# Squares of the attention output for three of four heads on GpSimd and VectorE instead of ScalarE, with the norm's chain issued in the next head's first unit

## Chip, cores, metric

The kernel runs on one core of a Trainium2 chip. The metric is the time of one execution on the device in microseconds (us); runs are compared by their median. TensorE (PE in the profile) multiplies matrices and transposes, VectorE (DVE), ScalarE (ACT) and GpSimd (POOL) do the elementwise work, SyncE (SP) issues most of the loads.

## The reference

Two layers. Each normalises its input, projects it, runs three groups of heads side by side (a recurrence, a gated convolution, an attention), multiplies each group's output by a gate and projects back. The change lies in the attention: 4 heads, 512 latent rows with 256 context rows, and two score matrices per head whose softmaxes are subtracted. What a head gives is normalised by the root of its mean square over the head's 128 values, and multiplied by a gate from `z`:

```python
def diff_attend(q, k, v, lam, scale):
    s = jnp.einsum('bqhjd,bkhjd->bhjqk', q, k).astype(jnp.float32) * scale
    p = jax.nn.softmax(s, axis=-1)
    attn = p[:, :, 0] - lam * p[:, :, 1]
    return jnp.einsum('bhqk,bkhe->bqhe', attn.astype(v.dtype), v)

    def finish(o, z):
        o = rms_norm(o, subln_g) * (1.0 - lam_init)
        return o.reshape(o.shape[0], o.shape[1], D_ATTN) * jax.nn.silu(z)
```

Layer 0 computes latent and context rows (768), layer 1 latent rows alone (512).

## The kernel before

The attention of a layer works through heads 0 to 3, and in each head through units of query tiles of 128 rows. Layer 0 has six tiles in five units, in the order `(0,), (4, 5), (1,), (2,), (3,)`: a unit is one latent tile against 768 keys or the two context tiles against 256 keys each. Layer 1 has four units of one tile.

The loop over units is a pipeline written out by hand. In the turn of unit u it transposes u's weights (`aT_mm` into the PSUM tile `aTp`, copied by ScalarE to `aT`), drains the output of the unit before (`drain`), makes the coefficient `cf` of the unit after it and combines that unit's two softmaxes with it (`coef`, `combine`: `e` on VectorE, and for a latent unit the 256 context columns on GpSimd, L1255 and L1256), takes the exponentials of the unit after that (`expo`), the scores `sc` and their row maxima `mx` of the one after that (`scores`, `maxi`), and multiplies u's weights by the values (`av`). TensorE's instructions, ScalarE's and those of VectorE that go through `dv` keep the order in which they are written. The small steps of the norm on VectorE and the work on GpSimd are placed between them by the tile scheduler.

`drain` copies a tile's output from PSUM to the head's tile O (L1298), and a second instruction of ScalarE squares it from PSUM and adds each row up into a column of `ss` (printed as `oss`). The squares themselves go to a tile `osq` that nobody reads.

`finish(h, O)` is the head's norm and gate, in two parts, run for head h within head h+1. Part 1 is issued at the end of the turn whose number in the head is FI: it loads the gate of the head from memory into the tile `zT`, of which there is one buffer, then makes `r0` (printed `r`), multiplies `oss` by it twice, scales, takes an inverse root (`rsqrt`: an integer estimate `rs_i`, `rs_y`, and three Newton rounds of three instructions with `rs_t`, the last result being `ors`), multiplies that by `r`, and scales O by it: on GpSimd for heads 0 to 2, on VectorE for head 3. Part 2 is issued at the end of turn FI2 = 3: TensorE transposes O into `oT`, in two groups; VectorE multiplies them by the gate in place in `zT`; ScalarE casts the result (`lat`, `ctx`), and GpSimd subtracts for the low part.

`aTp`, `av` and `oT` share two PSUM buffers. So `oT` waits for the reads of the `av` or `aTp` that had its buffer, and the `aTp` behind it for VectorE's reading of `oT`. Between these, output weights are split into high and low parts (`split`: `wo..hi` on ScalarE, `wo..lo` on GpSimd or VectorE, placed by the scheduler).

Of the kernel before, what the change touches and what calls it, by code (L numbers as in the profile page):

```python
# [10 lines left out]
F32 = mybir.dt.float32  # L11
# [3 lines left out]
ALU = mybir.AluOpType  # L15
AX = mybir.AxisListType
PSUM = bass.MemoryType.PSUM

P = 128
# [15 lines left out]
WH = 3  # L35
FSB = 3
PTB = 4
FI = 1
FK = (0,1,2,3,4,5,6,7)
HS = 0  # L40
WK = 2
# [65 lines left out]
def build(tc, A):  # L107
    nc = tc.nc
    ctx = ExitStack()
    S, G = nc.scalar, nc.gpsimd  # L110
# [17 lines left out]
    V = Vec()  # L128
# [63 lines left out]
    def small(n, tag, pool=None, bufs=2):  # L192
        return (pool or sm).tile([P, n], F32, tag=tag, bufs=bufs, name=tag)
# [5 lines left out]
    for l in range(L):  # L199
        t = cst.tile([P, NCC], F32, name=f"chan{l}")  # L200
# [260 lines left out]
    def fill(us):  # L461
        while us > 0 and fq:
            try:
                us -= next(fq[0])
            except StopIteration:
                fq.pop(0)
# [715 lines left out]
    def attention(l, lat, cx, pool, az_done, hd0):  # L1182
        last = l == L - 1
        li = 0.8 - 0.6 * math.exp(-0.3 * l)
        n = NL if last else NT
# [7 lines left out]
        ntt = 4 if last else 6  # L1193
        vA = pool.tile([P, 6, 512], F32, name="vA")
        ss = small(24, "oss", pool, 1)
# [11 lines left out]
        def dv(i):  # L1207
            order("v", i)

        def ac(i):  # L1210
            order("s", i)
# [81 lines left out]
        def drain(u):  # L1293
            for po, tt in zip(u["po"], u["tt"]):
                if AC & 4:
                    dv(V.tensor_copy(Os[u["h"]][:, tt], po))
                else:
                    ac(S.copy(Os[u["h"]][:, tt], po))  # L1298
                osq = pool.tile([P, P], F32, tag="osq", bufs=2, name="osq")
                col = u["h"] * 6 + tt  # L1300
                ac(S.activation(osq, po, AF.Square, accum_out=ss[:, col:col + 1]))

# [1 line left out]

        def finish(h, O):
            zT = pool.tile([P, NT], F32, tag="zT", bufs=ZB, name="zT")
            nc.sync.dma_start(out=zT[:, :n], in_=zd[l][h, :, :n])
            E1 = V if h == 3 else G
            c0 = h * 6
# [3 lines left out]
            for _ in range(2):  # L1313
# [6 lines left out]
                             in1=rs[:, :ntt].unsqueeze(2).to_broadcast([P, ntt, P]), op=ALU.mult)  # L1320
# [27 lines left out]
        def at(i):  # L1348
            return us[i] if 0 <= i < len(us) else None

        for x in range(-3, len(us)):
            u, p, c, e, w = at(x), at(x - 1), at(x + 1), at(x + 2), at(x + 3)
# [9 lines left out]
            if p:  # L1362
                drain(p)
# [25 lines left out]
            else:  # L1389
                fill(FA[1])  # L1390
            if u and u["i"] == FI and u["h"]:
                fins.append(finish(u["h"] - 1, Os[u["h"] - 1]))
# [82 lines left out]
    for l in range(L):  # L1475
        F.update(FL[l])
        last = l == L - 1
        n = NL if last else NT
# [248 lines left out]
```

## Time and profile before

| | |
|---|---|
| runs | 1145.35, 1146.66, 1151.25 us |
| median | 1146.66 us |
| profiled execution | 1148.92 us |
| its span in the profile | 1147.1 us |
| TensorE's mean granted clock | 0.97 of full speed |
| attention of layer 0 | about 476 to 574 us of the span |
| attention of layer 1 | about 1015 to 1094 us |

The span runs from the first to the last instruction; the 1.8 us between it and the profiled execution lie outside the instructions. Lines are read as start, duration, engine, line of the kernel, operation, tile written<-tiles read. `L118`, `L135`, `L137` and `L145` are helpers through which all of VectorE's, the matrix products' and the transposes' instructions pass, so there the tile's name tells what is done. A value in brackets is the time that the engine stood idle before the instruction, with what ended it.

### The profile page before, as it was taken

To read this page: it belongs to the slowest core of one execution; us is meant where nothing else is said; L and a number is where in the kernel's file an instruction comes from. 1 tells how busy PE (TensorE), PEld (TensorE's weight loads), DVE (VectorE), ACT (ScalarE), POOL (GpSimd) and SP (SyncE) were. 2 spreads that over 40 slices of the span, in tenths; PEclk is the share of its full clock that TensorE was granted. 3 is DMA by queue.
4 is the path that set the end of the run, shared out by engine and by line. 5 is a ranking of instruction groups with operands and counts; after the bars stand their busy time and mean duration, and the time that the engine had idled before them with its cause. 6 is when DMAs were issued, how large, how long until landed. Compare 5 with 4: busy or idle time off the path is not lost.

```text
span 1147.1 us, 25449 instructions
## 1 busy us (share of the span) xinstructions
PE 1038.8 (91%) x9850; PEld 849.6 (74%) x9850; DVE 721.3 (63%) x1704; ACT 523.4 (46%) x1330; POOL 499.2 (44%) x516
## 2 busy tenths in 40 slices
PE   4899989999799998988899998998988999888897
PEld 1577978777688867877787776866767887777775
DVE  3431458788567261589847867766885815479944
ACT  4323453453353222468724664654344433238731
POOL 1211444434726522555522345254475463456532
PEclk9889999999899999989999999999999999899999
DMA  9455231212424466653052452232223345555143
GB/s 356 174 194 167 80 89 57 57 35 70 139 75 130 139 189 187 195 170 102 15 188 80 142 186 78 84 83 76 79 71 103 103 133 149 154 164 165 47 156 110
DMA packets 92088, 142.55 MB, mean 124 GB/s; under 512 B 28192, under 2 KB 36416, under 8 KB 91968
## 3 DMA queue, kind: packets, MB, share of 16 engines
q1 hardware_dynamic: 88512, 136.14, 38.3%
q10 hardware_dynamic: 3456, 4.80, 1.2%
q8 instruction: 77, 1.26, 0.5%
q14 instruction: 43, 0.35, 0.1%
HBM read 110.99 MB, written 25.71 MB: 119 GB/s over the span
## 4 chain that ended last, share of the span: by engine, by line
PE 35%; DVE 21%; ACT 7%; POOL 6%; issue 5%; DMA 4%; SPq 1%; DVEq 0%; POOLq 0%; ACTq 0%
PE pcl L137 10%; PE op L137 6%; PE ptl L137 3%; DVE mx L118 3%; PE pcc L137 3%; PE ptc L137 2%; DVE rs_t L118 2%; POOL wlo L264 2%; PE av L137 1%; DVE e L118 1%; PE ch L135 1%; DVE bk L118 1%; DMA mraw<-in_mod_w_dram 1%; PE sc L137 1%; DMA qks<-qkr 1%
## 5 line engine op out<-in xcount | busy, mean ns | idle before, releaser
L264 POOL TENSOR_TENSOR wlo<-wraw,whi 128x512 fp32r<-128x512 f32 x134 | 182.0, 1361 | 310.4 <-ACT whi L261 265.7
L137 PE MATMUL pcl<-lat,whi 128*128 128x512 f32 (+1 forms) x928 | 300.1, 400 | 1.7 <-POOL lat L347 1.3
L137 PEld LDWEIGHTS pcl<-lat,whi 128*128 128x128 f32 x928 | 173.4, 193 | 44.1 <-issue 9.2
L137 PE MATMUL pcl<-lat,wlo 128*128 128x512 f32 (+1 forms) x464 | 187.8, 405 | 5.6 <-POOL wlo L264 3.7
L261 ACT CAST whi<-wraw 128x512 fp32r<-128x512 f32 x144 | 88.7, 619 | 159.8 <-DMA wraw<-in_w_in_dram 55.3
L137 PE MATMUL pcc<-ctx,whi 128*128 128x256 f32 x576 | 109.5, 286 | 2.0 <-DVE ctx L118 1.7
L137 PEld LDWEIGHTS pcl<-lat,wlo 128*128 128x128 f32 x464 | 89.7, 193 | 27.1 <-POOL wlo L264 5.6
L137 PEld LDWEIGHTS pcc<-ctx,whi 128*128 128x128 f32 x576 | 92.5, 192 | 8.4 <-issue 3.0
L137 PE MATMUL pcc<-ctx,wlo 128*128 128x256 f32 x288 | 83.3, 289 | 1.9 <-DVE wlo L118 1.9
L137 PE MATMUL ptl<-whi,lat 128*128 128x256 f32 x384 | 80.3, 296 | 0.0
L1244 ACT ACTIVATE e<-sc,mx 128x768 f32<-128x768 f32 (+1 forms) x80 | 66.3, 831 | 19.5 <-DVE mx L118 14.1
L118 DVE TENSOR_REDUCE mx<-sc 128x1 f32<-128x768 f32 (+1 forms) x72 | 63.7, 918 | 15.9 <-PE sc L137 15.9
L137 PE MATMUL av<-vA,aT 128*128 128x128 f32 x416 | 59.9, 288 | 14.0 <-ACT aT L1279 13.8
L137 PEld LDWEIGHTS av<-vA,aT 128*128 128x128 f32 x416 | 54.7, 197 | 20.9 <-ACT aT L1279 17.8
L137 PEld LDWEIGHTS ptl<-whi,lat 128*128 128x128 f32 x384 | 64.0, 198 | 2.0 <-issue 0.4
L137 PEld LDWEIGHTS pcc<-ctx,wlo 128*128 128x128 f32 x288 | 55.3, 192 | 5.1 <-issue 2.6
L118 DVE TENSOR_TENSOR R<-s,cs 128x384 f32<-128x384 f32 (+1 forms) x96 | 47.0, 529 | 18.6 <-PE s L135 17.8
L941 POOL TENSOR_TENSOR pz<-zu,pc 64x128 f32<-64x128 f32 x88 | 39.4, 448 | 42.1 <-DVE zu L118 37.4
L137 PE MATMUL ptl<-wlo,lat 128*128 128x256 f32 x192 | 56.5, 294 | 0.0
L137 PE MATMUL sc<-KH,QS 128*128 128x256 f32 (+1 forms) x144 | 52.0, 374 | 4.7 <-ACT e L1244 2.9
L137 PE MATMUL sc<-KL,QS 128*128 128x256 f32 (+1 forms) x144 | 45.7, 339 | 0.0
L1255 POOL TENSOR_TENSOR e<-e,cf 128x256 f32<-128x256 f32 x32 | 26.2, 819 | 42.1 <-DVE cf L118 14.1
(450 smaller groups left out, 2450.2 us busy)
## 6 DMA issues: line engine op xcount, KB each, us to landing
wraw<-in_w_in_dram SPq DMA_DIRECT2D x144, 256.0 KB, 2.7
mraw<-in_mod_w_dram SPq DMA_DIRECT2D x96, 256.0 KB, 4.3
KH<-qd SPq DMA_DIRECT2D x32, 192.0 KB, 3.9
oraw<-in_w_out_dram SPq DMA_DIRECT2D x20, 256.0 KB, 3.9
qd<-qks SPq DMA_DIRECT2D x12, 384.0 KB, 2.3
qd<-qkr SPq DMA_DIRECT2D x12, 384.0 KB, 2.5
qks<-qkr SPq DMA_DIRECT2D x64, 64.0 KB, 2.1
zu<-vd SPq DMA_DIRECT2D x96, 32.0 KB, 2.2
```

The source lines that it names most:

```text
L118: i = f(*a, **k)
L135: tc.keep_in_program_order(nc.tensor.matmul(*a, **k))
L137: i = nc.tensor.matmul(*a, **k)
L261: S.copy(hi, raw)
L264: eng.tensor_tensor(out=lo, in0=raw, in1=hi.bitcast(F32), op=ALU.subtract)
L941: G.tensor_tensor(out=pz[d][hr], in0=zu[d][hr, :, h, :], in1=prepd[d][1][hr, :, cc[d][1]].unsqueeze(2).to_broadcast([64, 2, HD]), op=ALU.mult)
L1244: ac(S.activation(ej[:, c], pb[:, c], AF.Exp, bias=mx[:, i:i + 1], accum_out=den[:, u["h"] * 6 + tt, j:j + 1]))
L1255: G.tensor_tensor(out=e1, in0=e1, in1=cf[:, 0:1].to_broadcast([P, NC]), op=ALU.mult)
```

## The change

ScalarE squares the tiles of head 3 alone. For heads 0 to 2, `finish` starts with a product of O with itself on GpSimd, written into the head's `zT`, and a sum of each 128 values on VectorE into `ss`; after these the gate is loaded into the same buffer. FI goes from 1 to 0, so part 1 is issued at the end of the next head's first turn, the one in which the head's last tile is drained. The tile `osq` has one buffer instead of two.

```diff
-FI = 1
+FI = 0
...
                 else:
                     ac(S.copy(Os[u["h"]][:, tt], po))
-                osq = pool.tile([P, P], F32, tag="osq", bufs=2, name="osq")
+                if u["h"] < 3:
+                    continue
+                osq = pool.tile([P, P], F32, tag="osq", bufs=1, name="osq")
                 col = u["h"] * 6 + tt
                 ac(S.activation(osq, po, AF.Square, accum_out=ss[:, col:col + 1]))
...
         def finish(h, O):
             zT = pool.tile([P, NT], F32, tag="zT", bufs=ZB, name="zT")
+            if h < 3:
+                sq = zT[:, :n].rearrange("p (t c) -> p t c", c=P)
+                G.tensor_tensor(out=sq, in0=O[:, :ntt], in1=O[:, :ntt], op=ALU.mult)
+                V.tensor_reduce(out=ss[:, h * 6:h * 6 + ntt], in_=sq, axis=AX.X, op=ALU.add)
             nc.sync.dma_start(out=zT[:, :n], in_=zd[l][h, :, :n])
             E1 = V if h == 3 else G
```

In numbers: 30 squares of 128x128 with their accumulator reads leave ScalarE (18 in layer 0, 12 in layer 1), and GpSimd gets six products and VectorE six sums (three over 128x768, three over 128x512).

The scheduler places some instructions anew. VectorE at the start of head 2 of layer 0, before (`oss` is the sum of squares, `e` with x2 the combine of the unit of two context tiles, `r` the reciprocal):

```order
L118 RECIPROCAL cf<-oden 128x2
L118 SCALAR_TENSOR_TENSOR cf<-cf,lm_579,oden 128x2
L118 TENSOR_TENSOR oss<-oss,r_6473 128x6
L118 SCALAR_TENSOR_TENSOR e_6363<-e_6377,cf,e_6363 128x256 x2
L118 TENSOR_TENSOR oss<-oss,r_6473 128x6
L118 TENSOR_SCALAR oss<-oss 128x6
L118 TENSOR_SCALAR rs_i<-oss 128x6
L118 TENSOR_SCALAR rs_y<-rs_i 128x6
L118 TENSOR_TENSOR rs_t<-rs_y 128x6
L118 TENSOR_REDUCE mx<-sc 128x1 x2
```

and now:

```order
L118 RECIPROCAL cf<-oden 128x2
L118 SCALAR_TENSOR_TENSOR cf<-cf,lm_579,oden 128x2
L118 SCALAR_TENSOR_TENSOR e_6343<-e_6357,cf,e_6343 128x256 x2
L118 TENSOR_REDUCE oss<-zT 128x6
L118 TENSOR_REDUCE mx<-sc 128x1 x2
L118 TENSOR_TENSOR oss<-oss,r_6413 128x6
L118 RECIPROCAL cf<-oden 128x1
L118 TENSOR_TENSOR oss<-oss,r_6413 128x6
```

The sum of the squares stands between the combine and the row maxima; the five steps that stood ahead of the maxima come behind them.

VectorE at the end of the same head, before (`e_6520` is the combine of its fifth unit, `e_6562` that of the next head's first; the numbers of buffers differ between the two kernels):

```order
L118 TENSOR_REDUCE mx<-sc 128x1
L118 TENSOR_TENSOR ors<-ors,r_6473 128x6
L118 TENSOR_REDUCE mx<-sc 128x1
L118 RECIPROCAL cf<-oden 128x1
L118 RECIPROCAL r_6732<-oden 128x6
L118 SCALAR_TENSOR_TENSOR cf<-cf,lm_579,oden 128x1
L118 SCALAR_TENSOR_TENSOR e_6520<-e_6533,cf,e_6520 128x512
L118 TENSOR_REDUCE mx<-sc 128x2 x2
L118 RECIPROCAL cf<-oden 128x1
L118 SCALAR_TENSOR_TENSOR cf<-cf,lm_579,oden 128x1
L118 TENSOR_TENSOR zT<-oT,zT 128x384
L118 SCALAR_TENSOR_TENSOR e_6562<-e_6577,cf,e_6562 128x512
```

and now, with `e_6494` for the fifth unit and `e_6534` for the next head's first:

```order
L118 SCALAR_TENSOR_TENSOR e_6494<-e_6507,cf,e_6494 128x512
L118 SCALAR_TENSOR_TENSOR ors<-rs_t,rs_y 128x6
L118 TENSOR_REDUCE mx<-sc 128x2
L118 TENSOR_TENSOR ors<-ors,r_6413 128x6
L118 TENSOR_REDUCE mx<-sc 128x2
L118 RECIPROCAL cf<-oden 128x1
L118 SCALAR_TENSOR_TENSOR cf<-cf,lm_579,oden 128x1
L118 SCALAR_TENSOR_TENSOR e_6534<-e_6549,cf,e_6534 128x512
L118 TENSOR_TENSOR zT<-oT,zT 128x384 x2
```

The last step of the inverse root stands behind the combine of the fifth unit, its product with `r` between the two maxima behind that, and both products with the gate behind the combine of the next head's first unit. TensorE's order is the same in both kernels.

GpSimd in the same head, from the middle, before (each pair of L1255 and L1256 belongs to one unit):

```order
L1255 TENSOR_TENSOR e_6464<-e_6464,cf 128x256
L1256 TENSOR_TENSOR e_6452<-e_6452,e_6464 128x256
L1319 TENSOR_TENSOR O<-O,ors 128x768
L1255 TENSOR_TENSOR e_6533<-e_6533,cf 128x256
L1256 TENSOR_TENSOR e_6520<-e_6520,e_6533 128x256
L1255 TENSOR_TENSOR e_6577<-e_6577,cf 128x256
L1256 TENSOR_TENSOR e_6562<-e_6562,e_6577 128x256
```

and now:

```order
L1255 TENSOR_TENSOR e_6466<-e_6466,cf 128x256
L1256 TENSOR_TENSOR e_6454<-e_6454,e_6466 128x256
L1255 TENSOR_TENSOR e_6507<-e_6507,cf 128x256
L1256 TENSOR_TENSOR e_6494<-e_6494,e_6507 128x256
L1325 TENSOR_TENSOR O<-O,ors 128x768
L1255 TENSOR_TENSOR e_6549<-e_6549,cf 128x256
L1256 TENSOR_TENSOR e_6534<-e_6534,e_6549 128x256
```

The scaling of O stands behind the pair of the fifth unit, where it stood ahead of it.

In head 1 of layer 1 `ors` and its product with `r` stood next to each other behind the combine of the next head's first unit; now one `mx` stands between them. In head 2 of layer 1 they stood on either side of the combine of the head's fourth and last unit; now they stand on either side of the combine of the next head's first. In head 3 of layer 0 the scaling of O keeps its place, and in head 3 of layer 1 `ors` still follows the last combine.

On SyncE's queue the gate's load for head 0 of layer 0 stands behind the loads of head 2 and ahead of one input weight and the loads of head 3; before, it stood ahead of the loads of head 2's rotary operands. Around the start of layer 0's attention GpSimd makes the low part `wo00lo` ahead of a rotary product `qks*sinT` instead of behind it.

## Rows read from the trace of the kernel before

**Rows 1.** The page's first part: busy time, share of the span and instructions of each engine.

```profile
PE 1038.8 (91%) x9850; PEld 849.6 (74%) x9850; DVE 721.3 (63%) x1704; ACT 523.4 (46%) x1330; POOL 499.2 (44%) x516
```

**Rows 2.** Busy time of each engine in the two stretches that the attention takes, layer 0 and layer 1, with the mean granted clock, the DMA share and GB/s.

```profile
core 0: us, PE busy (x) PEld busy (x) DVE busy (x) ACT busy (x) POOL busy (x), PEclk, DMA share, GB/s
476.00:574.00 98.00, 85.59 (x580) 76.00 (x579) 85.16 (x182) 71.58 (x224) 54.00 (x55) 0.97 0.36 106
1015.00:1094.00 79.00, 64.54 (x447) 56.77 (x446) 70.49 (x146) 54.85 (x153) 45.73 (x48) 0.98 0.38 110
```

**Rows 3.** The chain of work that ended last, in order of time, through head 2 of layer 0 (start, duration, engine, tile, line).

```profile
535.85 0.88 DVE e L118 x2
...
546.79 0.88 DVE mx L118
...
550.34 0.28 ACT osq L1301 x2
...
550.66 0.55 PE oT L145 x3
551.21 0.54 PE aTp L145 x3
...
555.44 0.27 ACT O L1298
555.71 0.28 ACT osq L1301 x2
...
556.01 0.04 DVE oss L118
...
556.09 0.88 DVE e L118 x2
...
557.87 1.73 DVE mx L118 x2
```

**Rows 4.** VectorE in order of time in the same head: start, duration, operation, out<-in, shapes, and in brackets the idle time before it with what ended it.

```profile
544.05 1.19 DVE L118 SCALAR_TENSOR_TENSOR e<-e,cf,e 128x512 f32<-128x512 f32 x1
545.16 0.69 DVE L118 SCALAR_TENSOR_TENSOR ors<-rs_t,rs_y 128x6 f32<-128x6 f32 x1
...
546.64 0.15 DVE L118 TENSOR_TENSOR ors<-ors,r 128x6 f32<-128x6 f32 x1
546.71 0.94 DVE L118 TENSOR_REDUCE mx<-sc 128x1 f32<-128x768 f32 x1
...
547.76 0.59 DVE L118 SCALAR_TENSOR_TENSOR cf<-cf,lm,oden 128x1 f32<-128x1 f32 x1
548.39 0.75 DVE L118 SCALAR_TENSOR_TENSOR e<-e,cf,e 128x512 f32<-128x512 f32 x1
549.06 1.28 DVE L118 TENSOR_REDUCE mx<-sc 128x2 f32<-128x512 f32 x2
...
550.58 0.55 DVE L118 TENSOR_TENSOR zT<-oT,zT 128x384 f32<-128x384 f32 x1
...
553.51 1.82 DVE L118 TENSOR_REDUCE mx<-sc 128x1 f32<-128x768 f32 x2 [1.07 <-PE sc L137]
```

**Rows 5.** GpSimd in order of time in the same head.

```profile
544.08 0.61 POOL L1255 TENSOR_TENSOR e<-e,cf 128x256 f32<-128x256 f32 x1 [2.50 <-DVE rs_t L118]
...
546.87 1.47 POOL L1319 TENSOR_TENSOR O<-O,ors 128x768 f32<-128x768 f32 x1 [1.04 <-DVE ors L118]
```

**Rows 6.** TensorE in order of time in layer 1, where the output of head 0 is finished in head 1.

```profile
1058.04 0.66 PE L145 MATMUL oT<-ident,O 128*128 128x128 f32 x4 [1.25 <-POOL O L1319]
1059.24 0.55 PE L145 MATMUL aTp<-ident,e 128*128 128x128 f32 x3 [0.54 <-DVE zT L118]
```

**Rows 7.** VectorE at the same place of layer 1.

```profile
1055.99 0.69 DVE L118 SCALAR_TENSOR_TENSOR ors<-rs_t,rs_y 128x4 f32<-128x4 f32 x1
1056.71 0.16 DVE L118 TENSOR_TENSOR ors<-ors,r 128x4 f32<-128x4 f32 x1
```

**Rows 8.** The tile osq, into which ScalarE writes its squares (L1301; the other lines of that name belong to another stage): count and min/median/max ns, and who waited for the tile, in us and times.

```profile
L1301 ACT ACTIVATE osq<-av x40: 271/283/348, 496.4 to 1093.1; 128x128 f32<-128x128 f32 x40
L1301 ACT ACTIVATION_READ_ACCUMULATOR osq<-av x40: 193/205/270, 496.6 to 1093.2; 128x1 f32 x40
...
  PEld aTp L145: 4.1, 8
...
  DVE oss L118: 3.6, 3
...
  PEld oT L145: 3.2, 5
```

**Rows 9.** GpSimd in layer 0's attention, grouped by line and shape (count | busy us, mean ns | idle us before).

```profile
L1319 POOL TENSOR_TENSOR O<-O,ors 128x768 f32<-128x768 f32 x3 | 4.4, 1469 | 2.6 <-DVE ors L118 2.3 <-DVE cf L118 0.3
```

**Rows 10.** The same for VectorE.

```profile
L118 DVE TENSOR_REDUCE mx<-sc 128x1 f32<-128x768 f32 x30 | 27.5, 948 | 4.1 <-PE sc L137 4.1
...
L118 DVE TENSOR_REDUCE mx<-sc 128x2 f32<-128x512 f32 x8 | 5.1, 683 | 0.5 <-PE sc L137 0.5
```

**Rows 11.** The issues of SyncE's DMA queue in layer 0's attention.

```profile
518.88 0.45 SPq L1178 DMA_DIRECT2D KH<-qd  x1
...
525.35 0.59 SPq L1179 DMA_DIRECT2D KL<-qd  x1
```


## Prediction

> **What bounds the kernel now.** The page's first part comes first: TensorE is busy for 91% of the span [rows 1], so a change on ScalarE, VectorE and GpSimd can matter only in a stage where TensorE waits. Then the busy times of the two attention stages [rows 2]. There TensorE is busy 85.6 of 98 us and 64.5 of 79, VectorE 85.2 and 70.5, ScalarE 71.6 and 54.9, GpSimd 54.0 and 45.7: VectorE is as full as TensorE, and ScalarE, which the change relieves, has more room than VectorE, which it loads. Then the chain through one head of layer 0 [rows 3]: the same place (the first `e` pair of a head) is passed at 535.85 and at 556.09, so a head takes 20.24 us, and the end of a stage moves by what is added to that period. ScalarE's squares (`osq`) stand in this chain twice a head with 0.28 us each: at 550.34, ahead of the transposes `oT`, and at 555.71, ahead of the norm's first `oss`. Most of the chain is VectorE's row maxima `mx` and combines `e`, in a fixed order, and at the end of a head `oT`, `zT` and the next `aTp`.
>
> **What is removed.** Thirty squares with their accumulator reads leave ScalarE: 283 and 205 ns each [rows 8], 0.28 us net of overlap in the chain [rows 3]. Thirty times that is 8.4 us of ScalarE time, but only the two places per head are on the path: 6 x 2 x 0.28 = 3.4 us at most. The first place is 0.28 us ahead of `oT`, the second is replaced by a longer wait, below. In all, `aTp`, `oss` and `oT` waited 4.1 + 3.6 + 3.2 = 10.9 us for `osq` [rows 8], and most of that is the `av` ahead of it, which stays.
>
> **What is added, at a head's start (term A).** GpSimd must square O, 128x768 in layer 0 and 128x512 in layer 1, and VectorE must sum it. No row shows a square on GpSimd; the nearest, its scaling of the same tile, takes 1.47 us [rows 5, 9]. Nor is there a sum from SBUF: a maximum over 128x768 takes 0.95 us, one over 128x512 0.68 [rows 10]; I take these. The squares need the last copy of O, which ends at 555.71 [rows 3]. Beside them runs the `e` pair of 0.88 us. If both overlap freely, the squares end at 557.2 and the sum at 558.2; if they exclude each other, both end about 555.7 + 1.47 + 0.88 = 558.1 and the sum at 559.05. The order now has that sum directly ahead of the pair `mx` that began at 557.87, and the five small steps that stood between `e` and `mx` (0.9 us from 556.97) stand behind it. So `mx` begins +0.4 to +1.2 us later, up to +1.5 with semaphores; I take **+0.9 per head** in layer 0 and +0.7 in layer 1, where both pieces are two thirds as long.
>
> That they exclude each other is seen elsewhere: VectorE's tiny `cf` began at 547.76 and ended at 548.35, with GpSimd's scaling of O, which ran from 546.87 to 548.34, while the `mx` of 546.71 beside the same scaling took 0.94 us, its usual time [rows 4, 5, 10]. [...]
>
> **What moves, at a head's end (term B).** The norm's chain starts later, since it needs the sum, and it is long: two `oss`, scale, `rs_i`, `rs_y`, nine steps of Newton, the last of which writes `ors`, `ors` times `r`, then GpSimd's scaling of O. VectorE's order weaves it between `mx` and `e`. Before, `ors` followed the `e` of the fourth unit (544.05) and the scaling of O ended at 548.34, ahead of its use [rows 4, 5]. In the new order it follows the `e` of the fifth, and GpSimd's scaling stands behind the fifth unit's pair. TensorE's order is the same: `oT` ahead of the fifth unit's `aTp`.
>
> Take X, the end of the `mx` at 546.79 + 0.88 = 547.67. Before, `aTp` began at 551.21, X + 3.5 [rows 3]. Now come after X: some six small steps, 0.5; `e`, 1.19 beside GpSimd's pair as at 544.05; `ors`, 0.62 net as at 545.16; a `mx` of two tiles, 0.64; `ors` times `r`, 0.15; GpSimd's scaling, 1.47; 0.15 of issue. That is X + 4.7. During the scaling `cf` is shut out as at 547.76, and the order has that `cf` and the next head's `e` (0.75) ahead of `zT` (0.55) [rows 4]. `aTp` needs the bank that the first `zT` frees. So `aTp` begins at X + 6.1, **+2.5 us**. With nothing in contention (`e` 0.75, `ors` 0.15, fewer small steps) it is X + 4.6, +1.1; with the second `e` in contention too, +3.0. What is late next is the scores behind `aTp`, for which VectorE already waited 1.07 us at 553.51: no slack takes this up.
>
> **The sum.** Layer 0: the ends of heads 0 and 1, finished in heads 1 and 2, cost 0.9 + 2.5 each, 6.8 (3 to 9). That of head 2, in head 3, keeps its place in the order and costs term A alone, 1.1. The start of the attention, where a rotary product on GpSimd falls behind a weight's low part, is 0 (-1 to +1.5). Together 8. Layer 1: `oT` already waited 1.25 us for the scaling of O, and `aTp` 0.54 for `zT`, in head 1 [rows 6]. There the order puts one `mx` (0.95, 0.87 net of overlap) between `ors` and `ors` times `r`, which stood together [rows 7]: 0.7 + 0.9 = 1.6. Head 2's finish now falls where head 1's was, and earns the same two waits: 0.7 + 1.8 = 2.5. Head 3: 0.7. Together 4.8, with 0.6 off for the low part of an output weight that VectorE makes earlier, outside this stretch: 4.2. In all **+12 us** (+5 if all bounds are low, +17 if nearly all are high). The profiled run took 1148.92 us, 1.8 more than its span and 2.3 over the median, and would be 1160.9; from the median, 1146.66 + 12 = about 1158.5.
>
> The Trainium skill (Perfetto Trace Analysis, section "Optimizing Scalar/DVE Operations") advises to move work to ScalarE when VectorE is saturated, and doubts moves between GpSimd and VectorE. The change does the reverse. By that advice alone, with the order left as it was, the sums cost VectorE 3 x 0.95 + 3 x 0.68 = 4.9 us, an estimate that is rival 2.
>
> **What is covered.** The load of zT now waits on SyncE's queue for the sum, since the squares use its buffer. Behind it stand one input weight and the loads of head 3, which were issued from 518.9 to 525.4 [rows 11]. The sum of head 0 falls one period before that of 557 to 559, at 518, and head 3's operands aren't used before head 2's start at 535.85, so this costs nothing; it would if the sum came more than some 8 us late. Its own use, the multiplication `zT`, is 15 us behind.
>
> **Rivals.**
> 1. Relief of ScalarE wins. The squares leave the chain, `av`'s bank comes free 0.28 us earlier, GpSimd squares in its idle time (2.50 us at 544.08 alone, [rows 5]) and the sum falls into VectorE's waits for `sc`, 4.1 us in layer 0 [rows 10]. It decides if the scaling of O is still ready when `oT` comes. Then -3.4 to -5: 1142 to 1143; all 10.9 us of waits for `osq` would be 1136. Against it: `oss` waited only 0.22 to 0.3 us for `osq`, and the sum is ten times as long as what it replaces on that path.
> 2. Only term A is paid: VectorE reaches the small steps early and the chain's end stays hidden. 2 x 0.9 + 1.1 + 3 x 0.7 = 5, so 1151 to 1152.
> 3. Contention is dearer: every small step beside GpSimd takes 0.6, as `ors` did, not 0.15, or head 3's loads come late. +17 to +22: 1164 to 1169.
>
> **How the numbers follow.** Forecast (+8 to +17) 0.54; rival 2 (+2 to +8) 0.23; rival 1 (-10 to +2) 0.16; rival 3 0.07. Half a per cent, about what a measurement of this kernel can tell from no change, is 5.7 us. Of rival 1 more than half passes it, 0.1; half of rival 2 (0.12) and the rest of rival 1 (0.06) lie within, 0.18; slower keeps 0.72. The range, with a tenth left out at each end, is 1147 to 1165.
>
> **What would show it.** Right: the period of heads 1 and 2 of layer 0 grows from 20.2 to about 23.5 us; a reduction of `oss` from `zT` stands ahead of `mx` and waits for GpSimd; `oT` waits on GpSimd's scaling of O by 1 us or more in heads 1 and 2 of both layers; `cf` beside it takes about 1 us. Wrong in term B: `oT` waits for `av` or ScalarE alone, and the period grows by under 1.5 us. Wrong altogether: the period shrinks, or the time appears outside the attention.

## The result: 1.4% slower

The changed kernel took 1160.82 us in the median of six runs (1157.0 to 1163.31), the kernel before, on the same chips, 1145.84 (1140.41 to 1151.25): a ratio of 1.0137, interval 1.0106 to 1.0167, so some 15.7 us more (12 to 19). The profiled execution took 1157.99 us with a span of 1156.2.

The spans of the two profiled executions lie only 9.1 us apart, though. Where the rest is can be read by cutting both at the same instructions. ScalarE's last copy of O in each head (L1298) does for that; the period of a head is the time from one head's last copy to the next's.

| us | head 0, first to last copy | head 1 | head 2 | head 3 | sum |
|---|---|---|---|---|---|
| layer 0 before | 18.42 | 20.51 | 20.24 | 17.76 | 76.93 |
| layer 0 after | 17.34 | 24.01 | 23.55 | 18.08 | 82.98 |
| layer 1 before | 12.82 | 15.74 | 19.54 | 16.54 | 64.64 |
| layer 1 after | 12.81 | 18.65 | 21.86 | 18.84 | 72.16 |

The attention takes 13.6 us more, 6.1 in layer 0 and 7.5 in layer 1. The 4.5 us by which the spans differ less lie outside it: the first copy came 1.4 us earlier (494.92 against 496.27) and the stretch from layer 0's last copy to layer 1's first was 2.9 us shorter. Over the profiled executions of all kernels below the first copy falls anywhere from 490.1 to 504.3 us, with the same instructions ahead of it, so that part tells nothing of the change. The attention is what to read.

VectorE in head 2 of layer 0 of the changed kernel, in order of time (start, duration, operation; in brackets the idle time before):

```profile
536.86 1.30 DVE L118 SCALAR_TENSOR_TENSOR cf<-cf,lm,oden 128x2 f32<-128x2 f32 x1
538.27 0.88 DVE L118 SCALAR_TENSOR_TENSOR e<-e,cf,e 128x256 f32<-128x256 f32 x2
539.07 0.94 DVE L118 TENSOR_REDUCE oss<-zT 128x6 f32<-128x768 f32 x1
539.93 1.81 DVE L118 TENSOR_REDUCE mx<-sc 128x1 f32<-128x768 f32 x2
...
547.76 0.94 DVE L118 TENSOR_REDUCE mx<-sc 128x1 f32<-128x768 f32 x1
...
549.81 0.58 DVE L118 SCALAR_TENSOR_TENSOR ors<-rs_t,rs_y 128x6 f32<-128x6 f32 x1
...
550.91 0.28 DVE L118 TENSOR_TENSOR ors<-ors,r 128x6 f32<-128x6 f32 x1
...
551.90 0.85 DVE L118 SCALAR_TENSOR_TENSOR cf<-cf,lm,oden 128x1 f32<-128x1 f32 x1
552.87 1.19 DVE L118 SCALAR_TENSOR_TENSOR e<-e,cf,e 128x512 f32<-128x512 f32 x1
553.98 1.01 DVE L118 TENSOR_TENSOR zT<-oT,zT 128x384 f32<-128x384 f32 x2
558.19 1.82 DVE L118 TENSOR_REDUCE mx<-sc 128x1 f32<-128x768 f32 x2 [3.19 <-PE sc L137]
```

GpSimd and TensorE beside it:

```profile
536.68 1.47 POOL L1311 TENSOR_TENSOR zT<-O 128x768 f32<-128x768 f32 x1 [1.83 <-ACT O L1298]
...
551.27 1.47 POOL L1325 TENSOR_TENSOR O<-O,ors 128x768 f32<-128x768 f32 x1
```

```profile
552.80 0.88 PE L145 MATMUL oT<-ident,O 128*128 128x128 f32 x6 [1.71 <-POOL O L1325]
554.58 0.55 PE L145 MATMUL aTp<-ident,e 128*128 128x128 f32 x3 [0.91 <-DVE zT L118]
```

In the kernel before, the row maxima behind the last copy of 555.71 [rows 3] in the same view, and TensorE at the head's end:

```profile
557.78 1.82 DVE L118 TENSOR_REDUCE mx<-sc 128x1 f32<-128x768 f32 x2
```

```profile
550.66 0.55 PE L145 MATMUL oT<-ident,O 128*128 128x128 f32 x3 [0.30 <-ACT osq L1301]
```

The product starts as soon as the last copy is done and takes 1.47 us. A `cf` of 128x2 that stands in VectorE's queue beside it, 0.22 us elsewhere, takes 1.30 and ends with it at 538.15. Then the `e` pair, then the sum, then the row maxima: they begin 3.4 us after the last copy of O (536.54), where they began 2.1 us after it. At the head's end the `mx` ends at 548.70, and `aTp` begins at 554.58, 5.9 us later; it was 3.5 [rows 3]. `oT` waits 1.71 us for the scaling of O, where it waited 0.3 for `osq`, and the wait of `mx` for the scores grows from 1.07 [rows 4] to 3.19 us.

Where the period is lost can be read by counting from the last copy of O of the head before (its start) to the same instructions in both kernels. The row X is the end of the `mx` from which the prediction counts its X (in head 2 at 547.65 us before and 548.70 after).

| us from the period's start, layer 0 | head 1 before | head 1 after | head 2 before | head 2 after |
|---|---|---|---|---|
| X | 12.64 | 12.91 | 12.45 | 12.44 |
| `aTp` behind `oT` begins | 16.31 | 18.79 | 15.99 | 18.31 |
| the next `mx` begin | 18.57 | 22.68 | 18.30 | 21.91 |
| the last copy of O, the period's end | 20.51 | 24.01 | 20.24 | 23.55 |

At X the later start is made up: 0.3 us of it are left in head 1 and nothing in head 2. Nearly all of the 3.5 and 3.3 us comes behind X: 2.2 and 2.3 us up to `aTp`, 1.6 and 1.3 more up to the next maxima, less 0.6 and 0.3 up to the last copy.

One thing follows that the prediction hadn't: the clock. Three stretches of the changed kernel, during that wait and behind it, and one of the kernel before, behind the same transposes (length, busy us and instructions of PE, PEld, DVE, ACT and POOL, granted clock, DMA share, GB/s):

```profile
551.00:553.00 2.00, 0.29 (x3) 0.21 (x3) 1.85 (x5) 0.27 (x1) 1.74 (x3) 1.00 0.00 0
553.00:557.00 4.00, 3.09 (x19) 2.72 (x17) 1.99 (x3) 1.78 (x6) 2.27 (x3) 0.78 0.00 0
557.00:559.00 2.00, 2.00 (x11) 1.81 (x10) 0.81 (x1) 1.74 (x7) 1.26 (x2) 0.59 0.00 0
```

```profile
551.00:555.00 4.00, 3.67 (x26) 3.11 (x25) 2.93 (x5) 3.17 (x11) 3.13 (x4) 1.00 0.01 2
```

TensorE worked 0.29 us of the first 2 us, and in the next 6 the mean granted clock is 0.78 and then 0.59 of full speed: part of the time it stood at the lower of its two levels, 1.2 GHz in place of 2.4. In the kernel before the clock is 1.00. Over the period of head 2 TensorE's busy time for the same 132 matrix instructions goes from 18.01 to 19.47 us, so up to 1.5 of the 3.3 us can be of this kind. It falls where the table shows the second part of the loss, between `aTp` and the next maxima.

In layer 1 the costly place is another. In order of time, after: ScalarE's last copy of O in head 1, then GpSimd from there on, then VectorE at two places.

```profile
1061.54 0.27 ACT L1298 COPY O<-av 128x128 f32<-128x128 f32 x1
```

```profile
1062.45 1.04 POOL L1325 TENSOR_TENSOR O<-O,ors 128x512 f32<-128x512 f32 x1 [1.03 <-DVE ors L118]
1065.30 0.61 POOL L1255 TENSOR_TENSOR e<-e,cf 128x256 f32<-128x256 f32 x1 [1.81 <-DVE cf L118]
1065.99 1.06 POOL L1256 TENSOR_TENSOR e<-e,e 128x256 f32<-128x256 f32 x1
1067.01 1.27 POOL L1339 TENSOR_TENSOR lat<-zT,lat 128x512 fp32r<-128x512 f32 x1
1068.36 1.04 POOL L1311 TENSOR_TENSOR zT<-O 128x512 f32<-128x512 f32 x1
```

```profile
1043.92 1.52 DVE L118 TENSOR_TENSOR qkr<-qkr,qks 128x512 f32<-128x512 f32 x1 [0.31 <-POOL qks L1118]
...
1069.43 0.69 DVE L118 TENSOR_REDUCE oss<-zT 128x4 f32<-128x512 f32 x1 [2.98 <-POOL zT L1311]
```

The last copy of head 1's O is done at 1061.81, but the product starts at 1068.36: it writes into zT, the only buffer of that name, and head 0's gated output is read from there until 1068.28. In VectorE's queue the sum stands ahead of the row maxima, so they wait too. The same happens a head later (2.99 us). By the first row maxima behind the sum 1.5 us are lost in head 2 and 2.4 in head 3, of 2.3 us each over the period. In head 1 there is no earlier reader; there the product (1043.85 to 1044.88) holds up a rotary sum (`qkr`), 1.52 us where it took 0.69:

```profile
1042.10 0.69 DVE L118 TENSOR_TENSOR qkr<-qkr,qks 128x512 f32<-128x512 f32 x1 [0.31 <-POOL qks L1118]
```

### The profile page after: what moved, and what is told of

Same layout as the page of the kernel before. It is cut to its first block, busy times and chain, and to the rows that moved or that the text cites. A ratio compares the mean times of both kernels' runs of the same rounds, so it can differ in the third digit from the quotient of the medians.

```text
span 1156.2 us, 25408 instructions
## 1 busy us (share of the span) xinstructions
PE 1037.2 (90%) x9850; PEld 849.7 (73%) x9850; DVE 725.3 (63%) x1710; ACT 517.7 (45%) x1270; POOL 507.3 (44%) x522
## 5 line engine op out<-in xcount | busy, mean ns | idle before, releaser
L137 PE MATMUL pcl<-lat,whi 128*128 128x512 f32 (+1 forms) x928 | 296.9, 397 | 1.0 <-POOL lat L347 0.8
L118 DVE TENSOR_REDUCE mx<-sc 128x1 f32<-128x768 f32 (+1 forms) x72 | 64.2, 917 | 17.3 <-PE sc L137 17.3
L137 PEld LDWEIGHTS av<-vA,aT 128*128 128x128 f32 x416 | 55.5, 198 | 23.7 <-ACT aT L1279 20.6
L137 PE MATMUL sc<-KH,QS 128*128 128x256 f32 (+1 forms) x144 | 54.5, 391 | 7.5 <-ACT qkr L1112 4.6
L118 DVE TENSOR_TENSOR R<-s,cs 128x384 f32<-128x384 f32 (+1 forms) x96 | 47.0, 529 | 18.7 <-PE s L135 17.9
L1255 POOL TENSOR_TENSOR e<-e,cf 128x256 f32<-128x256 f32 x32 | 29.6, 925 | 48.5 <-DVE oss L118 13.2
L137 PE MATMUL sc<-KL,QS 128*128 128x256 f32 (+1 forms) x144 | 48.1, 353 | 0.0
```

The source lines that it names most:

```text
L118: i = f(*a, **k)
L137: i = nc.tensor.matmul(*a, **k)
L1255: G.tensor_tensor(out=e1, in0=e1, in1=cf[:, 0:1].to_broadcast([P, NC]), op=ALU.mult)
```

## The experiments

Medians and ratios are against runs of the kernel before on the same chip. The intervals are 0.3 to 0.5% to each side, some 4 us, so kernels a few us apart can't be told apart by their ratios. The head periods show more, but each is read from one execution. Where the order and the granted clock are the same they repeat closely (heads 1 and 2 of layer 0 in e4 and e5: 18.72 and 18.73, 20.72 and 20.73). With the order the same and the clock not, they can differ: head 1 of layer 1 took 18.65 us in the changed kernel at a clock of 1.00, and at 0.91 it took 19.24 in e4 and 18.65 in e7. The last column is the sum of the two attentions' periods in the profiled execution, minus that of the kernel before (141.57 us).

| kernel | median us | ratio (95%) | L0 heads 0 to 3 | L1 heads 0 to 3 | attention |
|---|---|---|---|---|---|
| changed | 1160.82 | 1.0137 (1.0106, 1.0167) | 17.34 24.01 23.55 18.08 | 12.81 18.65 21.86 18.84 | +13.6 |
| e1 | 1149.65 | 1.0046 (1.0013, 1.0078) | 17.36 21.24 19.80 19.83 | 12.84 16.71 19.79 16.55 | +2.6 |
| e2 | 1150.03 | 1.0049 (1.0019, 1.0079) | 18.90 21.58 20.97 19.03 | 12.82 17.15 21.24 16.04 | +6.2 |
| e3 | 1164.03 | 1.0156 (1.0107, 1.0205) | 17.99 24.62 23.30 18.58 | 12.31 17.86 23.15 17.24 | +13.5 |
| e4 | 1156.08 | 1.0113 (1.0072, 1.0154) | 19.78 18.72 20.72 21.24 | 12.94 19.24 21.77 18.25 | +11.1 |
| e5 | 1155.34 | 1.0097 (1.0068, 1.0127) | 17.97 18.73 20.73 21.77 | 12.91 19.25 22.17 18.83 | +10.8 |
| e6 | 1155.19 | 1.0100 (1.0065, 1.0135) | 17.43 22.81 22.90 19.79 | 12.82 16.71 22.59 17.87 | +11.4 |
| e7 | 1160.09 | 1.0136 (1.0098, 1.0174) | 17.97 24.06 23.72 18.29 | 12.56 18.65 23.28 17.19 | +14.2 |
| e8 | 1149.56 | 1.0044 (1.0013, 1.0075) | 18.34 18.57 21.45 23.17 | 12.30 15.78 19.52 16.56 | +4.1 |
| e9 | 1159.96 | 1.0129 (1.0092, 1.0167) | 18.67 24.84 23.17 18.35 | 12.81 18.64 20.85 15.88 | +11.6 |
| e10 | 1158.40 | 1.0118 (1.0082, 1.0153) | 19.02 23.68 21.92 18.03 | 12.97 19.36 20.30 19.22 | +12.9 |
| e11 | 1159.33 | 1.0114 (1.0078, 1.0151) | 18.89 24.79 22.83 19.00 | 12.82 19.07 20.38 16.29 | +12.5 |
| e12 | 1150.64 | 1.0044 (1.0009, 1.0079) | 18.35 21.31 21.59 17.76 | 12.43 16.63 20.44 17.47 | +4.1 |

**e1, the turn alone.**

```diff
-FI = 1
+FI = 0
```

> The kernel before with FI = 0 alone: ScalarE still squares all heads, and the norm's chain is issued in the next head's first turn. In its order ors times r stands one to two units earlier than in the kernel before, not later. Theory (the sum of squares delays the chain, and so its end comes after oT needs O): no cost, ratio to the kernel before 0.995 to 1.002, and oT waits for GpSimd's scaling of O nowhere in layer 0. Rival 1 (issuing the chain in the first turn is itself what costs, by putting its small steps and the gate's load in the way): 1.005 to 1.015. Rival 2 (GpSimd's square and VectorE's sum cost only by their own time, the place of the chain's end doesn't matter): ratio 0.998 to 1.002, and no shorter wait of oT anywhere.

The ratio is 1.0046, between the two theories. `oT` waits for the scaling of O nowhere in layer 0, as forecast, and head 2 is even 0.4 us shorter. But head 3 of layer 0 takes 2.1 us more. TensorE there, and the stretch around it (columns as above, the clock is the 0.59):

```profile
574.92 0.69 PE L145 MATMUL aTp<-ident,e 128*128 128x128 f32 x2 [0.43 <-POOL e L1256]
```

```profile
574.00:577.00 3.00, 2.41 (x11) 2.22 (x12) 1.38 (x2) 0.95 (x4) 2.61 (x4) 0.59 0.00 0
```

The earlier chain put GpSimd's scaling of O inside the pair of another unit, and that unit's transposes waited for the pair. TensorE's busy time in head 3 grows by 1.5 us for as many instructions (106), so the clock can be the larger part of the 2.1 us. The first turn does cost something, then, 2.6 us in the attention, by where it puts one instruction on GpSimd.

**e2 and e12, nothing in place of the squares.** In the changed kernel (e2), and in the kernel before with the same two lines in `drain` (e12):

```diff
-                sq = zT[:, :n].rearrange("p (t c) -> p t c", c=P)
-                G.tensor_tensor(out=sq, in0=O[:, :ntt], in1=O[:, :ntt], op=ALU.mult)
-                V.tensor_reduce(out=ss[:, h * 6:h * 6 + ntt], in_=sq, axis=AX.X, op=ALU.add)
+                V.tensor_tensor(out=ss[:, h * 6:h * 6 + ntt], in0=O[:, :ntt, 0], in1=O[:, :ntt, 0], op=ALU.mult)
```

> The changed kernel with the product on GpSimd and the sum on VectorE left out for heads 0 to 2: in their place VectorE squares one of the 128 values of each row (a step of 128x6), so the norm of these heads is not that of the reference. ScalarE is relieved as in the change. Against e1 this shows the relief of ScalarE alone, against the changed kernel the cost of the squares with all that hangs on it. Theory: the chain's end is early again, so the ratio to the kernel before is 0.990 to 0.999, 1 to 4 us under e1 (twelve places of 0.28 us at most, 3.4 us), and 13 to 20 us under the changed kernel. Rival 1 (the first turn costs): 1.003 to 1.012. Rival 2 (own time only): some 5 to 8 us under the changed kernel, 1.006 to 1.010.

> The kernel before (FI = 1) without ScalarE's squares of heads 0 to 2 and with nothing in their place but a step of 128x6 on VectorE that squares one of the 128 values of each row: the relief of ScalarE alone, with the chain about where it was (the scaling of O stands on GpSimd ahead of the same units as in the kernel before). The norm of these heads is not that of the reference. If ScalarE's squares cost what they show in the chain (0.28 us at twelve places), ratio to the kernel before 0.996 to 0.999, and 2 to 4 us less in the two attention stages. If what they free is taken up by other waits: 0.999 to 1.003. e2, the same with FI = 0, was at 1.005, so a relief of 1 us or more here would mean that the first turn costs some 6 us.

Both are slower than the kernel before, by 0.49 and 0.44%, though they do less. e2 misses the range of its theory and lies in that of the first turn, but e12, without the first turn, is as slow and lies above both of its ranges. In neither order does a relief of ScalarE show, and rival 1 of the prediction falls with that. In e12 head 3 of layer 0 has the period of the kernel before to the hundredth, so the single buffer that the change leaves to `osq` costs nothing there. Heads 1 and 2 lose 0.8 and 1.4 us, and in both `aTp` waits for `zT`, which it didn't before:

```profile
526.07 0.55 PE L145 MATMUL aTp<-ident,e 128*128 128x128 f32 x3 [1.31 <-DVE zT L118]
...
547.65 0.55 PE L145 MATMUL aTp<-ident,e 128*128 128x128 f32 x3 [1.54 <-DVE zT L118]
```

In head 2 the scheduler has put the first `zT` behind the next head's combine, where the kernel before had it ahead. That is the last piece of term B alone, without a late O and without a sum. In head 1 `zT` keeps its place, but the low part `wo21lo` (0.68 us) and a combine that took 1.95 us beside GpSimd's scaling of O come ahead of it:

```profile
522.40 1.95 DVE L118 SCALAR_TENSOR_TENSOR e<-e,cf,e 128x512 f32<-128x512 f32 x1
```

```profile
521.82 1.98 POOL L1323 TENSOR_TENSOR O<-O,ors 128x768 f32<-128x768 f32 x1 [2.18 <-DVE ors L118]
```

**e3, the squares with the old turn.** The changed kernel with `FI = 1`.

> The changed kernel with FI = 1: squares on GpSimd and the sum on VectorE, but issued one turn later. In its order ors times r stands at the same places as in the changed kernel in heads 1 and 2 of both layers, and later in head 3 of layer 1. Theory: the same late end, ratio to the kernel before 1.010 to 1.018. Rival 1 (FI = 0 is the cost): 0.998 to 1.005. Rival 2 (own time only): 1.004 to 1.008.

1.0156: as the theory of the late end had it, and against the turn as the main cause. TensorE's idle time before the transposes `oT` that is put down to GpSimd's scaling of O is 13.5 us in sum, against 7.1 in the changed kernel.

**e4, e5 and e8, a later part 2.** e4 is the changed kernel with

```diff
-            if u and u["i"] == FI2 and u["h"]:
+            if u and u["i"] == len(tts) - 1 and u["h"]:
```

e5 the same with `(len(tts) - 1 if u["h"] < 3 else FI2)`, and e8 that line in the kernel before.

> The changed kernel with the second part of finish (transposes oT, gate) in the turn of the head's last unit: in layer 0 one turn later, the fifth instead of the fourth; layer 1 unchanged. The sum, the product and the chain stay where they are. Theory: in heads 1 and 2 of layer 0 the wait of oT for GpSimd's scaling of O (1.71 us each) and of aTp for zT (0.91) go, the granted clock stays at 1.00 there, and the period of these heads falls from 23.5 to about 21.0 us: 4 to 6 us under the changed kernel, ratio to the kernel before 1.008 to 1.011. Rival 2 (own time only, the waits are slack that something else would take): the same as the changed kernel, 1.012 to 1.015.

> The changed kernel with part 2 of finish one turn later (the fifth unit) in heads 1 and 2 of layer 0 alone; head 3 keeps the fourth turn, unlike e4, where head 3 of layer 0 lost 3 us by it. Theory (the late end of the chain is paid at oT): periods of heads 1 and 2 of layer 0 fall from 24.0 and 23.6 us to 19 to 21, as in e4, head 3 stays near 18: layer 0 6 to 8 us under the changed kernel, ratio to the kernel before 1.006 to 1.010. Own-time theory (the product, the sum and the steps that they push back are what costs): periods of 21.5 to 22.5, 1.010 to 1.013.

> The kernel before with part 2 of finish one turn later in heads 1 and 2 of layer 0 alone (FI = 1, ScalarE squares all heads). If the place of oT matters only where O is late, this is 0 to 2 us faster than the kernel before (oT waited 0.3 us for osq there, aTp 0.3 for oT and zT): ratio 0.997 to 1.001. If a later part 2 is by itself cheaper or dearer, the periods of heads 1 and 2 (20.51 and 20.24 us) move by more than 0.7 us.

Head 1 of layer 0 falls to 18.7 us and head 2 to 20.7, and the granted clock is 1.00 in both, where it was 0.93. But a transposition that comes a turn later falls beyond the last copy, into the next head's period: head 3 takes 21.2 and 21.8 us. Over the layer e4 saves 2.5 us and e5 3.8, not 4 to 6 and 6 to 8. And e8 shows that the later part 2 by itself costs 4.6 us in layer 0 (81.53 against 76.93). Up to 1.2 us of that can be the clock: in head 3 it is 0.93, and TensorE is busy 18.03 us, against 16.87 for as many instructions at 1.00 in e5. So a later part 2 saves where O is late and costs where O is ready, 8 us apart in the same four heads; with part 2 late in both, the changed layer 0 is no longer the slower one (79.20 against 81.53).

**e6, squares that nobody waits for.** The kernel of e1 with

```diff
+            if u and u["i"] == 0 and u["h"]:
+                sq = pool.tile([P, 6, P], F32, tag="sqt", bufs=1, name="sqt")[:, :ntt]
+                G.tensor_tensor(out=sq, in0=Os[u["h"] - 1][:, :ntt], in1=Os[u["h"] - 1][:, :ntt], op=ALU.mult)
+                V.tensor_reduce(out=small(6, "sqd", pool, 1)[:, :ntt], in_=sq, axis=AX.X, op=ALU.add)
```

> The kernel of e1 (FI = 0, ScalarE squares all heads, the chain ends early) with the product of O on GpSimd and the sum on VectorE added for heads 0 to 2, into a tile and a column that nobody reads. Nothing waits for them, so it shows their own time and what they block. Theory: 0.5 to 1.0 us per head over e1, 3 to 6 us in all, ratio to the kernel before 1.006 to 1.010, and oT waits for GpSimd no more than in e1. Own-time theory: as slow as the changed kernel, 9 us and more over e1, 1.012 to 1.016.

1.0100, 6 us over e1 by the ratios, the upper edge of the forecast, and 8.8 by the periods, above it. By the periods the changed kernel is 11.0 over e1, so most of its loss comes back without an O that is late for `oT`. It isn't a clean measure of own time, since the pieces landed elsewhere. VectorE in head 2 of layer 0:

```profile
544.33 0.95 DVE L118 TENSOR_REDUCE sqd<-sqt 128x6 f32<-128x768 f32 x1 [1.74 <-POOL sqt L1396]
```

A sum whose result nobody needs still stops VectorE for 1.74 us, because it stands in the queue and its product is late: GpSimd had the scaling of O and half a pair ahead of it. Behind it `aTp` waits 1.76 us for `zT`, the same place as in the changed kernel and in e12.

**e7, O scaled on VectorE.**

```diff
-            E1.tensor_tensor(out=O[:, :ntt], in0=O[:, :ntt],
+            V.tensor_tensor(out=O[:, :ntt], in0=O[:, :ntt],
```

> The changed kernel with O scaled on VectorE for all heads (it was GpSimd for heads 0 to 2); the sum, the product and part 2 stay. VectorE scaled the last head's O in 0.96 us in layer 0 and 0.69 in layer 1, against 1.47 and 1.04 on GpSimd, and no cf waits for GpSimd any more. Theory (the end of the chain sets the time): oT comes some 0.7 to 1.2 us earlier in heads 1 and 2 of layer 0 and in heads 1 and 2 of layer 1, 2 to 5 us under the changed kernel, 1.009 to 1.012. Own-time theory (VectorE's load is what costs): 3 x 0.96 + 3 x 0.69 = 5 us more on VectorE, so 1.014 to 1.018.

No change (1.0136), against the forecast. VectorE in head 2 of layer 0 shows why:

```profile
551.94 0.28 DVE L118 TENSOR_TENSOR ors<-ors,r 128x6 f32<-128x6 f32 x1
552.15 0.68 DVE L118 TENSOR_REDUCE mx<-sc 128x2 f32<-128x512 f32 x1
552.75 0.94 DVE L118 TENSOR_TENSOR O<-O,ors 128x768 f32<-128x768 f32 x1
```

The scheduler put the scaling behind one more `mx`. It takes 0.94 us in place of 1.47 but starts 0.5 us later, and `oT` begins 1.9 us after `ors` times `r`, as in the changed kernel. In this head the end of the chain wasn't moved, so e7 doesn't decide between the two theories. Its ratio lies just under the range of the own-time theory.

**e9, e10 and e11, the buffer and the chain.** e9 gives the product a tile of its own:

```diff
-                sq = zT[:, :n].rearrange("p (t c) -> p t c", c=P)
+                sq = pool.tile([P, 6, P], F32, tag="sqt", bufs=1, name="sqt")[:, :ntt]
```

e10 puts the lines of `finish` from `s_, d_` to the scaling of O under

```diff
+            with tc.high_priority(offset=60):
```

and e11 does both.

> The changed kernel with the product in a tile of its own instead of zT, so that it need not wait until GpSimd has read the gated output of the head before from zT, and the gate's load need not wait for the sum. In layer 1 of the changed kernel the product of heads 1 and 2 began 6.5 us after the last copy of O, behind that reading, and the sum waited 2.98 and 2.99 us for it in VectorE's queue. Theory (late chain, and a sum that waits for the buffer): these two waits go, the periods of heads 2 and 3 of layer 1 fall by 2 to 3.5 us each, layer 0 moves by less than 1 us per head; 4 to 7 us under the changed kernel, ratio to the kernel before 1.007 to 1.011. Own-time theory: the same as the changed kernel, 1.012 to 1.016. If the load of the gate behind the sum held up SyncE's queue, layer 0 would gain too.

> The changed kernel with the same instructions, but the small steps of the norm's chain and the scaling of O given a higher priority in the scheduler. In its order each chain step comes one place earlier: in layer 0 ors stands ahead of the fifth unit's combine, its product with r right behind that, ahead of both maxima, and the products with the gate ahead of the next head's first combine; in layer 1 no maximum stands between ors and its product any more. Theory (the end of the chain sets oT and aTp): heads 1 and 2 of layer 0 fall from 24.0 and 23.6 us to 21.0 to 22.5, heads 1 and 2 of layer 1 by 0.5 to 1.5; 4 to 7 us under the changed kernel, ratio to the kernel before 1.007 to 1.011. Own-time theory: no change against the changed kernel, 1.012 to 1.016.

> e9 and e10 together: the product in its own tile, and the chain's steps with a higher priority. Theory: the two gains add, 8 to 13 us under the changed kernel, ratio to the kernel before 1.002 to 1.007; the rest is the sum and the product themselves at a head's start, 0.9 us a head. Own-time theory: 1.010 to 1.016.

e9: both waits of the sum for zT are gone from layer 1, head 2 falls by 1.0 us and head 3 by 3.0, to 15.88, under the kernel before. That is 4.0 us by the periods of layer 1. The clock over head 3 is 1.00, where it was 0.91, but the 3.0 us are won early in the head: the first row maxima behind the sum begin 5.1 us after the period's start, in place of 8.2. Layer 0 shows no gain (heads 1 and 2 together +0.5), so the gate's load held up nothing there. Over both layers the attention is only 2.0 us shorter, and the ratio, 1.0129, can't be told from the changed kernel's: it lies in the range of the own-time theory, not in that of the late chain.

e10: in layer 0 heads 1 and 2 fall by 0.3 and 1.6 us, to 23.7 and 21.9, where 21.0 to 22.5 was forecast for both. TensorE in head 1, then in head 2:

```profile
536.84 0.88 PE L145 MATMUL oT<-ident,O 128*128 128x128 f32 x6 [1.57 <-POOL O L1326]
538.04 0.85 PE L145 MATMUL aTp<-ident,e 128*128 128x128 f32 x3 [0.32 <-DVE zT L118]
...
559.75 0.87 PE L145 MATMUL oT<-ident,O 128*128 128x128 f32 x6 [1.56 <-POOL O L1326]
560.94 0.55 PE L145 MATMUL aTp<-ident,e 128*128 128x128 f32 x3 [0.32 <-DVE zT L118]
```

The wait of `aTp` for `zT` shrinks from 0.91 to 0.32 in both heads, but `oT` waits nearly as long as in the changed kernel (1.71): one place in the order isn't enough for a chain of some 15 steps that cannot start before the sum. The two heads have the same waits, and still the clock over head 1 is 0.93 and over head 2 1.00. From `aTp` to the next maxima head 1 takes 3.9 us and head 2 2.3, as in the kernel before. So what sets head 2 apart is the clock, and the earlier chain is worth 0.3 to 0.7 us a head, by which `aTp` comes earlier. The ratio, 1.0118, lies between the two ranges.

e11 keeps e9's gain in layer 1 (68.56 us, against 68.18 in e9 and 72.16 in the changed kernel) and adds nothing to it. In layer 0 it gains nothing. 1.0114 is far from the 1.002 to 1.007 of the theory and lies in the range of own time. No kernel here beats the kernel before, and none of the runs points to one.

## Why the prediction was right, and where it was off

**Direction and size.** Forecast +12 us with a range of 1147 to 1165, measured +15.7 (12 to 19), 1160.82. The likeliest case came true. Layer 0 was to cost 8 us and cost 6.1, layer 1 was to cost 4.2 and cost 7.5, so in the sum two errors partly cancel. Rival 1 is refuted by the ratio, and e2 and e12 show no relief either. The argument against it, that `oss` waited only 0.22 to 0.3 us for `osq`, left out the longest of the three waits in [rows 8], 3.2 us behind head 3 of layer 0, whose squares stay. Rival 2, term A alone, is refuted in layer 0 by the 1.71 us that `oT` waits, and by the ratio. Rival 3 gave 1164 to 1169 and is above the median measured; one of its parts, small steps that take 0.6 us beside GpSimd, is there in single rows (`ors` 0.58).

Of the signs named, the periods came, and the waits of `oT` (1.71 us in heads 1 and 2 of layer 0, 2.04 and 1.66 in layer 1), and a `cf` of 0.85 us beside the scaling. The sum waits for GpSimd in layer 1 alone; in layer 0 VectorE isn't idle before it.

**Term A in layer 0** was +0.9 per head; the maxima begin 1.3 us later. That is near the upper of the two ends worked out from the rows, the one where the product and VectorE's two-input instructions exclude each other. The `cf` of 1.30 us that ends with the product shows it. In heads 1 and 2 it was `cf` that lost the race, not the `e` pair; in head 3 the product began behind `cf`, and the `e` pair took 1.93 us. The Trainium skill (SBUF — State Buffer, section "Who interferes with whom") says that a VectorE instruction with two SBUF inputs contends with a GpSimd instruction that reads SBUF, and that on trn2 a reduction never contends. The rows agree on the reduction too: layer 1's sum at 1069.43 took 0.69 us though GpSimd began a subtraction at 1069.76, and the next one, at 1090.98 with GpSimd idle from 1090.95 on, took 0.69 as well.

But heads 1 and 2 didn't pay this term: at X, 0.3 us of it are left in head 1 and nothing in head 2. Fewer of the chain's steps now stand ahead of X. In head 2, besides, the two combines on the way took 0.75 us each, where they had taken 1.20 and 1.19: now GpSimd's multiplication beside them is the one that waits (1.11 us, where it took 0.62 and 0.61). The prediction added the later start to the later end, as if nothing between them could take it up.

**Term B in layer 0** was X + 6.1; measured X + 5.9, against 3.5. Its mechanism is there: the late scaling, then a `cf` that ends with it, then `zT`, then `aTp`. Inside it two races went the other way, the fifth unit's `e` taking 0.75 us instead of 1.19 and the next head's `e` 1.19 instead of 0.75, and they cancel. Heads 1 and 2 were to cost 3.4 us each and cost 3.5 and 3.3; the period was to be 23.5 and is 24.0 and 23.6. This agreement is luck in part: the sum had 0.9 for a start that isn't paid, and lacked the stretch from `aTp` to the next maxima, 1.6 and 1.3 us, in which the clock is low. e10 shows that this stretch is the clock's: with the clock at 1.00 it is as long as before. That the late O is paid there is shown by the cut at X, and by e4 and e5, which take the wait away, against e8. How much of it can be won back by a faster chain isn't shown: e7 and e10 hardly moved `oT`.

**Head 3 of layer 0** was to cost 1.1, which the prediction doesn't work out (term A is 0.9), and cost 0.3. The start, put at 0, can't be judged: head 0 of layer 0 takes 17.3 to 19.8 us in the fourteen profiles, without a pattern in what was changed.

**Term A in layer 1 is the step that failed:** "+0.7 in layer 1, where both pieces are two thirds as long". It sized the pieces and not what the product waits for. In heads 2 and 3 the sum waits 2.98 and 2.99 us for a product that waits for zT. Heads 1 to 3 cost 2.9, 2.3 and 2.3 us, not 1.6, 2.5 and 0.7. The text named the buffer only for the gate's load behind the product, not for the readers ahead of it. e9 gives the product another buffer, and both waits go, with 4.0 us of layer 1.

The 0.6 us taken off for a low part made earlier, outside this stretch, shows in no run. VectorE makes three low parts within heads 1 to 3 in both kernels; `wo01lo` moved from head 2 (1065.64) into head 1 (1051.13, 0.67 us), where it adds to the loss.

**Where it is paid.** `aTp` waits for `zT` 0.9 us in heads 1 and 2 of layer 0 of the changed kernel, 1.3 and 1.5 in e12, 1.4 and 1.8 in e6, and not at all in the kernel before. In e12 nothing is added, and in e6 O isn't late. What the three have in common is that VectorE comes late to `zT`.

**What the forecast didn't have:** e1, e8 and e12 change the place of steps without adding more than a step of 128x6, and each is 0.44 to 0.46% slower, about 5 us; e2, with no squares, is at 0.49%. By the ratios about a third of the 15.7 us is of this kind, and the product and the sum with what they delay are the other 10 (1.0137 against e2's 1.0049). The forecast put all of it on terms A and B. In e1 and e12 a row shows the place that pays; that a third of the change's own loss is made up of such places is an inference from the ratios.

**Open:** the reading of layer 0 rests on one execution of each kernel. By the ratios alone, e9 and e11 fall in the ranges of the own-time theory and e7 just under its range; against that theory speak the cut at X for layer 0, and for layer 1 the waits that e9 removes. What makes the clock fall in one head and not in another with the same waits isn't shown.

## What to carry to other kernels

Before moving work off an engine with room onto two others, ask what the result is waited for by: a sum in an in-order queue stops everything behind it, and here even one that nobody read cost 1.74 us. When a result is put into a buffer that exists once, size the wait for its earlier reader as its own term, in every stage apart, since the reader's distance differs between them. A later start isn't a later end: cut both kernels at the same instructions and see what is left of it before adding the two. And in a hand-ordered pipeline measure the reordering alone first: about 5 us came from each of three changes that added almost no work.

## What the runs showed of the hardware

A wait of 1.7 us of TensorE for O, with 0.9 us more behind it, was followed by a stretch at a mean granted clock of 0.78 (0.59 in e1 behind waits of 1.36, 0.30 and 0.43 us), and the same 132 matrix instructions took 1.5 us longer in that head. So a wait can be paid twice, though not each time. With waits of 1.6 and 0.32 us in both heads, e10 had a clock of 0.93 over head 1 and 1.00 over head 2. Where the transposes stood elsewhere (e4, e5), the clock stayed at 1.00 over heads 1 and 2 of layer 0.

A 128x2 coefficient on VectorE took 1.30 us beside GpSimd's product of 1.47 us, and ended with it; alone it takes 0.22. A step with a single input can be held up as well. `rs_i` read 128x6 of `oss` in 0.58 us and ended with the GpSimd instruction beside it; in the kernel before, with GpSimd idle, it took 0.17 us (537.04).

```profile
542.84 0.58 DVE L118 TENSOR_SCALAR rs_i<-oss 128x6 int32<-128x6 int32 x1
```

```profile
542.28 1.11 POOL L1255 TENSOR_TENSOR e<-e,cf 128x256 f32<-128x256 f32 x1 [4.13 <-DVE oss L118]
```
